# Every 16th output store of a gather, prefix-sum and matmul kernel goes out as two transfers, of 120 and of 8 partitions

## The chip, the core and the metric

The kernel runs on one core of a Trainium2 chip. The core has a matrix engine (PE, with its weight loads shown as PEld), a vector engine (DVE), a scalar engine (ACT), GpSimd (POOL) and a queue engine (SP) that here only issues transfers. The transfers themselves run on 16 DMA engines that all issuers share. Times are device microseconds (us) of one execution, and the figure that counts is the median over runs.

## The reference

```python
B, S, N, D = (16, 4096, 2048, 512)
# x: B x S x D float32, indices: B x N int64, sorted, w: D x D float32
b_idx = np.arange(B)[:, None]
gathered = x[b_idx, indices, :].copy()
cs = np.cumsum(gathered, axis=1)
return np.matmul(cs, w).astype(np.float32)
```

For each of 16 batches, 2048 rows of 512 floats are picked out of 4096, summed up along the rows (a running sum), and multiplied with a 512 x 512 matrix. 67.1 MB are gathered and 67.1 MB are written.

## The kernel before

The 16 x 2048 = 32768 gathered rows are cut into T = 256 tiles of 128 rows. Two tiles (R = 2) make a group, so there are G = 128 groups, 8 to a batch. A group's output is 256 rows of 2 KB, 512 KB.

The program is written by hand, engine by engine, with semaphores. The small class Lane (its method need waits on a semaphore only where that engine hasn't yet waited for as high a value) makes the waits. What follows is the way of one group.

GpSimd runs `gather(t)` for all 256 tiles, an indirect transfer that takes one row index per partition and brings 128 rows of 2 KB into `g32`. There are 16 such tile buffers (NG = 16, each with its own semaphore `s_g`), so a gather waits only for the cast of 8 groups before (`s_c`).

ACT runs `cast(g)` (L121), which turns a gathered group into float16, and `drain(g)` (L180), which copies a projected group out of PSUM into one of NO = 8 output buffers `ob`. Casts run three groups ahead of drains: cast(g + 3), drain(g), cast(g + 4), drain(g + 1) and so on. `drain(g)` waits for the store of the group 8 before it (`s_o`), so that the buffer is free, and for the projection (`s_b`).

PE runs `sums(t)` (L132), which makes the running sums inside a tile by multiplying with a triangle of ones, and `project(g, j)` (L168), the product with w. DVE runs `carry(t)` (L152, L147), which adds the last sum of the tile before and writes float16.

SP runs `store(g)` (L186) for all groups in order. It waits for `drain(g)` through `s_e` and issues one transfer of 128 partitions, 4 KB each, from `ob`. At the end SP waits for the last 8 stores. The order of the stores on SP and of the drains on ACT is the order of the groups. A transfer adds 16 in all to its semaphore when it has landed, which is why the waits count in sixteens.

The lines around the change, in short:

```python
def drain(g):
    act.need(s_o[g % NO], 16 * (g // NO))
    act.need(s_b, R * (g + 1))
    nc.scalar.copy(out=ob[g % NO][:], in_=pb[g % NB][:]).then_inc(s_e, 1)
...
    dst = out[b, h * R * P : (h + 1) * R * P, :].rearrange("(p j) d -> p j d", j=R)
    sp.need(s_e, g + 1)
    nc.sync.dma_start(out=dst, in_=ob[g % NO][:]).then_inc(s_o[g % NO], 16)
```

With j = R = 2, partition p holds the output rows 2p and 2p + 1 of the group, which lie one behind the other in memory: 4 KB in one piece for each partition.

Of the kernel before, what the change touches and what calls it, by code (L numbers as in the profile page):

```python
# [27 lines left out]
def kernel(  # L28
# [7 lines left out]
    nc = tc.nc  # L36
# [8 lines left out]
    G = T // R  # L45
# [5 lines left out]
    NA = 4  # L51
    NB = 2
    NC = 4
    NO = 8
    LOOP = 4
    AH = 2
# [16 lines left out]
    g16 = [const.tile([P, R, D], FP16, name=f"g16_{i}") for i in range(NH)]  # L73
    cst = [const.tile([P, DC, R, P], FP16, name=f"cst{i}") for i in range(NC)]
    ob = [const.tile([P, R, D], FP32, name=f"ob{i}") for i in range(NO)]
    pa = [ps.tile([P, DC, R, Q], FP32, name=f"pa{i}") for i in range(NA)]
# [4 lines left out]
    def sem(name):  # L81
        return tc.alloc_semaphore(name)
# [5 lines left out]
    s_g = [sem(f"s_g{i}") for i in range(NG)]  # L88
    s_o = [sem(f"s_o{i}") for i in range(NO)]
    s_c = sem("s_c")  # L90
    s_a = sem("s_a")
    s_d = sem("s_d")
    s_b = sem("s_b")
# [2 lines left out]
    pool, pe, dve, act, sp = (  # L96
        Lane(e) for e in (nc.gpsimd, nc.tensor, nc.vector, nc.scalar, nc.sync)
    )
# [42 lines left out]
    def carry(t):  # L141
        g, r = divmod(t, R)
        dve.need(s_b, R * (g - NC + 1))
        dve.need(s_a, t + 1)
        dst = cst[g % NC][:, :, :, r * Q : (r + 1) * Q]
        if t % NT == 0:
            nc.vector.tensor_copy(out=dst, in_=pa[t % NA][:]).then_inc(s_d, 1)  # L147
            return
        e = (r - 1) % R
        last = cst[(t - 1) // R % NC][:, :, R - 1, e * Q + Q - 1 : e * Q + Q]  # L150
        dve.need(s_d, t)
# [7 lines left out]
    def project(g, j, first=0):  # L159
# [7 lines left out]
        for c in range(DC):  # L167
            mm = nc.tensor.matmul(  # L168
                out=pb[g % NB][:, j],
                lhsT=cst[g % NC][:, c, j, :],  # L170
                rhs=w16[:, c, :],
# [4 lines left out]

    def drain(g):
        act.need(s_o[g % NO], 16 * (g // NO))
        act.need(s_b, R * (g + 1))
        nc.scalar.copy(out=ob[g % NO][:], in_=pb[g % NB][:]).then_inc(s_e, 1)  # L180

    def store(g):
        b, h = divmod(g, GB)
        dst = out[b, h * R * P : (h + 1) * R * P, :].rearrange("(p j) d -> p j d", j=R)
        sp.need(s_e, g + 1)
        nc.sync.dma_start(out=dst, in_=ob[g % NO][:]).then_inc(s_o[g % NO], 16)  # L186


    with nc.allow_non_contiguous_dma(reason="a few indices, one per partition"):
        nc.sync.dma_start(  # L190
            out=idx_first[:],
            in_=indices[0, 0 : FIRST * P].bitcast(U32).rearrange("(t p w) -> p t w", p=P, w=2),
        ).then_inc(s_first, 16)
    idx_rows = indices.bitcast(U32).rearrange("b (t q) -> (b t) q", q=2 * P)
    for k in range(KI):
        nc.sync.dma_start(
            out=idx64[:, k, :], in_=idx_rows[k * P : (k + 1) * P, :]
        ).then_inc(s_idx[k], 16)
    nc.sync.dma_start(out=w32[:], in_=w.rearrange("(c p) d -> p c d", p=P)).then_inc(s_w, 16)
    for g in range(G):  # L200
        store(g)
    for g in range(G - NO, G):
        sp.need(s_o[g % NO], 16 * (g // NO + 1))


    nc.gpsimd.memset(ident[:], 1.0).then_inc(s_ut, 1)  # L206
# [3 lines left out]
        out=ident[:],  # L210
        in_=ident[:],
# [7 lines left out]
        out=ut[:],  # L219
        in_=ut[:],  # L220
# [14 lines left out]
    for k in range(KI):  # L235
# [3 lines left out]
            out=pb[k % NB][:, 0, :P], in_=idxf[:, k, :], identity=ident[:]  # L239
# [31 lines left out]
    for g in range(G):  # L271
        if g + AH + 1 < G:
            cast(g + AH + 1)
        drain(g)
# [30 lines left out]
```

## Time and profile before

| what | value |
|---|---|
| median of 6 runs | 350.95 us (350.22 to 352.24) |
| the profiled execution: its time / its span | 352.32 us / 350.6 us |
| PE busy | 299.7 us (85%) |
| ACT busy | 253.4 us (72%) |
| POOL busy | 243.4 us (69%) |
| DVE busy | 178.1 us (51%) |
| DMA queue of GpSimd's gathers (q0) | 20480 records, 67.13 MB, 49.3% of 16 engines' span |
| DMA queue of SP's transfers (q1) | 19520 records, 68.43 MB, 48.4% |
| clock granted to PE | 0.999 |

The span is the time from the first to the last instruction of the profiled execution; its own time is 1.7 us longer and is one of a spread of runs. The share of busy time of an engine is a mean over the whole span. The page's name for a group of instructions is its line, engine, operation and the buffers it writes and reads ("g<-in_x_dram,idxg" is a gather). A DMA record is one packet that one of the 16 engines moves: 4 KB of data for gathers and stores, or 4 B for the write to a semaphore. Records overlap by a few ns where an engine is never idle, so that shares can add up to slightly more than 100%.

### The profile page before, as it was taken

What the parts mean: (1) busy time and instruction counts of PE and PEld (TensorE: products, weight loads), DVE (VectorE), ACT (ScalarE), POOL (GpSimd) and SP (SyncE); (2) the same over time, 40 slices, a digit from 0 to 9 for tenths busy, and PEclk for the clock granted to TensorE, in tenths of its full rate; (3) what the DMA queues carried; (4) which work ended last, traced back from release to release, by engine and by line L of the source; (5) the groups of instructions that cost most, each with busy time, mean ns of one, the idle gap of its engine ahead of it and who ended that gap; (6) DMA issues with size and microseconds to landing.
All of it is one profiled execution on the core that took longest, in us unless ns stands there. A gap on an engine that the chain in (4) does not pass through costs nothing.

```text
span 350.6 us, 6009 instructions
## 1 busy us (share of the span) xinstructions
PE 299.7 (85%) x2050; PEld 149.7 (43%) x2050; DVE 178.1 (51%) x260; ACT 253.4 (72%) x258; POOL 243.4 (69%) x264
## 2 busy tenths in 40 slices
PE   0498898898899889898998888998898998898993
PEld 0253443444444444444444444444444444444441
DVE  1364554464555546455554555555554555555550
ACT  0874877787787787776877767878787786877873
POOL 6777777777777777777777777777777777776000
PEclk9999999999999999999999999999999999999999
DMA  6789999999999999999999999999999999999845
GB/s 220 225 279 354 395 411 414 415 412 420 407 418 414 410 415 409 416 415 411 416 416 415 415 410 408 406 414 405 417 414 416 414 415 406 411 417 416 356 193 239
DMA packets 40012, 135.66 MB, mean 387 GB/s; under 512 B 6464, under 2 KB 6720, under 8 KB 40000
## 3 DMA queue, kind: packets, MB, share of 16 engines
q0 software_dynamic: 20480, 67.13, 49.3%
q1 hardware_dynamic: 19520, 68.43, 48.4%
q14 instruction: 11, 0.09, 0.1%
q8 instruction: 1, 0.02, 0.0%
HBM read 68.42 MB, written 67.11 MB: 387 GB/s over the span
## 4 chain that ended last, share of the span: by engine, by line
POOL 46%; DMA 27%; issue 18%; ACT 4%; PE 3%; POOLq 0%; SPq 0%; ACTq 0%
POOL g L109 46%; DMA g<-in_x_dram,idxg 26%; ACT g L121 3%; PE pb L168 3%; DMA g<-in_x_dram,idx_first 1%; PE pa L132 1%; DMA idx_first<-in_indices_dram 1%; ACT w L268 0%; ACT L121 0%; ACT ob L180 0%; POOLq L229 0%; ACTq L23 0%; SPq L300 0%; SPq L79 0%
## 5 line engine op out<-in xcount | busy, mean ns | idle before, releaser
L109 POOL DMA_INDIRECT g<-in_x_dram,idxg x254 | 240.2, 946 | 77.4 <-issue 71.3
L168 PE MATMUL pb<-w,cst 128*128 128x512 f16 x1024 | 263.6, 380 | 0.0
L152 DVE TENSOR_TENSOR cst<-pa,cst 128x512 f16<-128x512 f32 x240 | 166.0, 692 | 139.4 <-PE pa L132 138.4
L121 ACT CAST g<-g 128x1024 f16<-128x1024 f32 x128 | 133.6, 1045 | 78.8 <-issue 75.8
L132 PE MATMUL pa<-ut,g 128*128 128x128 f16 x1024 | 100.9, 222 | 40.9 <-ACT g L121 40.3
L180 ACT COPY ob<-pb 128x1024 f32<-128x1024 f32 x128 | 128.7, 1006 | 4.7 <-PE pb L168 4.7
L132 PEld LDWEIGHTS pa<-ut,g 128*128 128x128 f16 x1024 | 70.0, 99 | 128.6 <-ACT g L121 95.9
L168 PEld LDWEIGHTS pb<-w,cst 128*128 128x128 f16 x1024 | 89.9, 98 | 61.8 <-issue 1.1
L147 DVE CAST cst<-pa 128x512 f16<-128x512 f32 x16 | 11.1, 691 | 20.4 <-PE pa L132 20.4
L121 ACT ACT_TABLE_LOAD x1 | 1.3, 1283 | 9.5 <-DMA g<-in_x_dram,idx_first 9.5
L238 PE MATMUL pb<-ident,idxf 128*128 128x128 f32 x2 | 0.7, 458 | 4.6 <-DVE idxf L234 4.6
L109 POOL DMA_INDIRECT g<-in_x_dram,idx_first x2 | 2.1, 1060 | 1.6 <-DMA idx_first<-in_indices_dram 1.2
L234 DVE CAST idxf<-idx 128x128 f32<-128x128 uint32 x2 | 0.5, 228 | 4.4 <-DMA idx<-in_indices_dram 4.2
L238 PEld LDWEIGHTS pb<-ident,idxf 128*128 128x128 f32 x2 | 0.4, 182 | 4.7 <-issue 4.6
L268 ACT CAST w<-w 128x2048 f16<-128x2048 f32 x1 | 1.9, 1892 | 0.0
L243 DVE CAST idxg<-pb 128x128 uint32<-128x128 f32 x2 | 0.6, 290 | 0.3 <-PE pb L238 0.3
L206 POOL MEMSET ident<- 128x128 f32 x1 | 0.2, 204 | 0.5 <-SPq L79 0.5
L209 POOL TENSOR_SCALAR_AFFINE_SELECT ident<-ident 128x128 f32<-128x128 f32 x1 | 0.3, 286 | 0.1
L289 POOL MEMSET const-float32-0.0<- 128x1 f32 x1 | 0.1, 98 | 0.3 <-issue 0.3
L218 POOL TENSOR_SCALAR_AFFINE_SELECT ut<-ut 128x128 f16<-128x128 f16 x1 | 0.3, 289 | 0.0
L207 POOL MEMSET ut<- 128x128 f16 x1 | 0.2, 204 | 0.0
L289 POOL MEMSET const-uint8-127<- 128x1 uint8 x1 | 0.1, 115 | 0.0
(2 smaller groups left out, 0.2 us busy)
## 6 DMA issues: line engine op xcount, KB each, us to landing
out_dram<-ob SPq DMA_DIRECT2D x128, 512.0 KB, 6.9
g<-in_x_dram,idxg POOLq DMA_INDIRECT x254, 11.1
w<-in_w_dram SPq DMA_DIRECT2D x1, 1024.0 KB, 5.6
idx<-in_indices_dram SPq DMA_DIRECT2D x2, 128.0 KB, 2.6
g<-in_x_dram,idx_first POOLq DMA_INDIRECT x2, 5.1
idx_first<-in_indices_dram SPq DMA_DIRECT2D x1, 2.0 KB, 1.9
```

The costliest lines, as they stand in the source:

```text
L109: nc.gpsimd.indirect_dma_start(out=g32[g % (NG // R)][:, r, :], out_offset=None, in_=x_flat, in_offset=bass.IndirectOffsetOnAxis(ap=ap, ax ...
L121: nc.scalar.copy(out=g16[g % NH][:], in_=g32[g % (NG // R)][:]).then_inc(s_c, 1)
L132: mm = nc.tensor.matmul(out=pa[t % NA][:, c], lhsT=g16[g % NH][:, r, c * P : (c + 1) * P], rhs=ut[:], start=(c == 0), stop=(c == DC - 1),)
L147: nc.vector.tensor_copy(out=dst, in_=pa[t % NA][:]).then_inc(s_d, 1)
L152: nc.vector.tensor_tensor(out=dst, in0=pa[t % NA][:], in1=last.unsqueeze(2).broadcast_to([P, DC, R, Q]), op=mybir.AluOpType.add,).then_inc ...
L168: mm = nc.tensor.matmul(out=pb[g % NB][:, j], lhsT=cst[g % NC][:, c, j, :], rhs=w16[:, c, :], start=(c == 0), stop=(c == DC - 1),)
L180: nc.scalar.copy(out=ob[g % NO][:], in_=pb[g % NB][:]).then_inc(s_e, 1)
L209: nc.gpsimd.affine_select(out=ident[:], in_=ident[:], compare_op=mybir.AluOpType.is_equal, fill=0.0, base=0, pattern=[[-1, P]], channel_mu ...
L234: nc.vector.tensor_copy(out=idxf[:, k, :], in_=idx64[:, k, 0::2]).then_inc(s_if, 1)
L238: nc.tensor.transpose(out=pb[k % NB][:, 0, :P], in_=idxf[:, k, :], identity=ident[:]).then_inc(s_pt, 1)
L243: nc.vector.tensor_copy(out=idxg[:, k, :], in_=pb[k % NB][:, 0, :P]).then_inc(s_prep, 1)
L268: nc.scalar.copy(out=w16[:], in_=w32[:]).then_inc(s_wc, 1)
```

## The change

The store of every 16th group (0, 16, ..., 112) is issued as two transfers: the first 120 partitions, 480 KB, count on the buffer's semaphore as before; the last 8 partitions, 32 KB, count on a new semaphore, `s_o2`. The drain that will overwrite such a buffer (groups 8, 24, ..., 120) waits for both, and SP waits for `s_o2` once more at the end. Bytes, buffers, and the other 120 stores stay as they are.

```diff
+    SPLIT = 16
+    CUT = 120
...
+    s_o2 = sem("s_half")
...
     def drain(g):
         act.need(s_o[g % NO], 16 * (g // NO))
+        if (g - NO) % SPLIT == 0:
+            act.need(s_o2, 16 * max(0, (g - NO) // SPLIT + 1))
         act.need(s_b, R * (g + 1))
...
         sp.need(s_e, g + 1)
-        nc.sync.dma_start(out=dst, in_=ob[g % NO][:]).then_inc(s_o[g % NO], 16)
+        src = ob[g % NO]
+        if g % SPLIT:
+            nc.sync.dma_start(out=dst, in_=src[:]).then_inc(s_o[g % NO], 16)
+        else:
+            nc.sync.dma_start(out=dst[:CUT], in_=src[:CUT]).then_inc(s_o[g % NO], 16)
+            nc.sync.dma_start(out=dst[CUT:], in_=src[CUT:]).then_inc(s_o2, 16)
...
     for g in range(G - NO, G):
         sp.need(s_o[g % NO], 16 * (g // NO + 1))
+    sp.need(s_o2, 16 * ((G - 1) // SPLIT + 1))
```

## The prediction

> **What bounds the kernel now.** I read the chain of waits first, cut to its last 29 us. Columns: start in us, length in us, what was running.
>
> ```profile
> 321.97 0.30 issue
> 322.27 16.23 DMA g<-in_x_dram,idxg
> 338.50 0.72 issue
> 339.23 1.05 ACT g L121
> ...
> 345.36 1.01 ACT ob L180
> ```
>
> The reader is to see that the last gather is issued at 322.27, needs 16.23 us to land, and that everything after it (cast, sums, projection, the last copy, the last store) takes 350.6 - 338.5 = 12.1 us. So the end is "last gather landed" plus a fixed tail. Before it the chain is a row of gathers on GpSimd; the page's group for them:
>
> ```profile
> L109 POOL DMA_INDIRECT g<-in_x_dram,idxg x254 | 240.2, 946 | 77.4 <-issue 71.3
> ```
>
> 946 ns busy and 0.30 us of issue make 1.25 us for each gather, and 3.2 + 255 x 1.25 = 322 is exactly where the last one is issued: GpSimd is never held up. Hence only the landing time of the last gather can move the end earlier, down to GpSimd's own pace. Next I read the list of DMA issues in six windows of 20 us (20:40, 60:80, 120:140, 180:200, 240:260, 300:320), for the stores in the first and last, then the gathers in all six; the last number is the median us from issue to landing.
>
> ```profile
> out_dram<-ob SPq DMA_DIRECT2D x8, 512.0 KB, 6.9
> out_dram<-ob SPq DMA_DIRECT2D x8, 512.0 KB, 6.8
> g<-in_x_dram,idxg POOLq DMA_INDIRECT x17, 6.8
> g<-in_x_dram,idxg POOLq DMA_INDIRECT x17, 8.4
> g<-in_x_dram,idxg POOLq DMA_INDIRECT x17, 10.0
> g<-in_x_dram,idxg POOLq DMA_INDIRECT x17, 12.3
> g<-in_x_dram,idxg POOLq DMA_INDIRECT x17, 14.7
> g<-in_x_dram,idxg POOLq DMA_INDIRECT x17, 16.5
> ```
>
> Stores keep their time, gathers fall behind by 9.7 us over 280 us: the gather queue gets a backlog. Then the DMA view of 45:300, where the load is steady, and of two windows near the end, 331:335 and 335:339 (records, MB, share of 16 engines):
>
> ```profile
> DMA packets 30521, 105.28 MB, mean 413 GB/s; under 512 B 4831, under 2 KB 4831, under 8 KB 30513
> ```
> ```profile
> DMA  1111097997998979972101011010011029999999
> ...
> q1 hardware_dynamic: 224, 0.83, 51.3%
> q0 software_dynamic: 16, 0.05, 3.3%
> ```
> ```profile
> q1 hardware_dynamic: 217, 0.76, 47.0%
> q0 software_dynamic: 14, 0.05, 2.8%
> ```
>
> 413 GB/s over 16 engines is 25.8 GB/s each, or 4096 B in 158.7 ns. The windows near the end carry the case. Gathers are still outstanding (the last lands at 338.5), yet their queue uses 3.3% and then 2.8% of 16 engines, half of ONE engine (1/32 is 3.1%), and between the bursts of stores the busy row falls to 0 and 1 tenths. One gather gives each engine 4 packets of 4 KB and one semaphore write (20480 gather records / 256 gathers / 16 engines = 5). 16 records in 4 us are 3.2 gathers, one per 1.25 us: a single engine, alternating gather and store packets, while fifteen have finished their gathers. In 327:338.5 that queue has 63 records, in 327:331 34, of which that engine at its rate makes 16; the other 18 are less than one last gather of the others. So the late engine had about 63 - 18 = 45 records, 9 gathers, 36 packets, left when the others were done: 36 x 158.7 ns = 5.7 us of work. With equal numbers of store packets between, that is 11 us in time, and a gather counts as landed only when all engines are done.
>
> **What the Trainium skill says.** (1) Page "DMA: Bandwidth & Descriptors", section "Latency and other measured facts": of the 16 engines, numbers 7 and 15 are usually slower in traces. The trace agrees that one is late; it has no engine numbers, so which one it is stays open. (2) Same page, "Why a DMA increments its semaphore by 16 and not by 1": a transfer uses the largest k up to 16 that divides the slowest dimension of both sides, for a transfer issued from SP on the lowest-numbered k engines; of the semaphore's 16, the missing 16 - k are written at once. For 128 partitions k is 16, and the trace agrees in count (6464 records under 512 B, less 4096 of the gathers and 256 of the first indices, are 2112 = 132 transfers x 16). For smaller k no run here shows it yet. (3) Same page, "Rules for kernel authors", advises against cutting a transfer into two halves, as both use the same engines; that speaks against a gain from cutting as such, not against moving load between engines.
>
> **The change part by part.** Stores 0, 16, ..., 112 are cut: 8 of 128.
> - Load of the engines. Uncut, each engine gets 128/16 = 8 packets per store. By (2), 120 partitions give k = 15, 8 packets on engines 0 to 14 and none on 15; 8 partitions give k = 8, one packet on engines 0 to 7. Over 8 stores: engine 15 loses 64 packets, 64 x 158.7 = 10.2 us of work; engines 0 to 7 gain 8, 1.27 us; 8 to 14 keep theirs. Store 0 is issued at 20.1 us, before the transfers are saturated, so about 7 x 0.159 = 1.1 us counts.
> - If 15 is the late engine, 10.2 us is more than the 5.7 it is behind. It stops being last; engines 0 to 7 are next, 1.1 us above the level of the others: 5.7 - 1.1 = 4.6 us gained.
> - Cross-check by queue. With all engines equal, a gather and its half store are 8 packets, 8 x 158.7 = 1270 ns, against 1250 ns of GpSimd: 20 ns are still lost per gather, over the 220 gathers from 45 us on 4.4 us. The last gather would then take 6.8 + 4.4 + 1.1 = 12.3 us in place of 16.23: 3.9 us gained. The two ways give 3.9 and 4.6; I take 4.5, nearer to the count of packets, because the 6.8 us of the first window still holds transfers of the start.
> - Bounds. At best the saturated 158.7 ns shrink once nobody waits, GpSimd's 1250 ns set the pace and no backlog grows: 6.8 + 1.1 = 7.9 us for the last gather, 8.3 us gained. At worst nothing is gained here (rivals below).
> - SP: 8 more transfers at 332 ns each (the SP group's duration) beside 299 us in which SP waits for L180. The second piece leaves 0.33 us later than the first. Nobody reads it but the copy 8 groups later. Cost 0; without that cover 2.7 us.
> - ACT: 8 more waits (g = 8, 24, ..., 120), each on a store issued 8 groups before, some 20 us, and landing in 7. Queued behind is the copy at L180 and through it PE's next projection. ACT is idle 0.6 to 0.8 us ahead of most casts. The wait is always met; a waiting instruction shows as 0.02 us in the chain (ACTq L23), so 8 x 0.02 = 0.2 us, hidden. If a wait did bite it would be by the 0.33 us of the second issue, 2.6 us in all.
> - Last wait on SP: the last cut store is number 112, out 35 us before the end. Cost 0.
>
> Sum against the profiled execution: span 350.6 - 4.5 = 346.1. Its own time was 352.32, 1.4 over the median of 350.95, so I apply the difference to the median: 350.95 - 4.5 = 346.4.
>
> **Rivals.**
> A. The late engine is one of 0 to 7 (7 is the other engine that the skill names). It keeps all its work and gets 7 to 8 packets more: 1.1 to 1.3 us later, last gather and end with it; 352.2, slower. It decides from two packets over a late engine on. For: the skill names 7 and 15 alike. Against: it says that both are slow, and here only one is; nothing in the trace excludes it.
> B. The late engine is one of 8 to 14, or its lag comes from other traffic (the instruction queue moves 11 packets, 0.09 MB, in the span) that falls on an engine not relieved. Load on it unchanged: 350.9, same.
> C. The 120 partitions go out on 8 engines instead of 15. Then 0 to 7 get 15 + 1 packets per cut store, 8 more: 10.2 us in all. Even with the late engine freed it is 10.2 - 5.7 = 4.5 us slower, 355.4. Against: the rule in (2).
> D. The 120 partitions are spread over all 16 engines anyway; then nothing is relieved or loaded by more than a few packets: within 0.5 us, same.
>
> **How the numbers follow.** Forecast 0.58; A 0.18; B 0.10; C 0.08; D 0.04; 0.02 for a small gain in another way. What a measurement of this kernel can tell from no change is about 0.3%, 1.05 us. Faster: 0.58 + 0.02 = 0.60. Slower: A + C = 0.26. Same: B + D = 0.14. The likeliest case has its own range, 342.5 (the bound of 8.3 us) to 348.0 (a gain of 3). Adding B, D and A reaches to 352.4 and leaves out C and the edges: about 0.85 held, so the range is 342.5 to 352.4.
>
> **What would show it.** Right: the gathers' time to landing grows to 11 to 13 us in 300:320 instead of 16.5; the last gather lands near 334; near the end the gather queue no longer runs at half of one engine alone for 11 us, but several engines finish within some 2 us. The issue list shows 120 stores of 512 KB, 8 of 480 and 8 of 32, and the store queue has fewer semaphore records (15 + 8 per cut store). GpSimd's 1.25 us and the tail of 12 us stay. Wrong: 16 or more us to landing at the end with one engine still alone (A, B), or eight engines busy with gathers at the end, half of 16 (C).

## The result, and the profile after

The changed kernel takes 352.71 us (median of 16 runs, 351.43 to 354.19) against 351.42 us of the kernel before (37 runs, 350.22 to 353.0). The ratio is 1.0038, with a 95% interval from 1.0026 to 1.0050: 1.3 us slower, 0.9 to 1.8. The forecast was 346.4, and the range ended at 352.4.

The pair of profiled executions can't show this. Their spans are 350.8 and 350.6 us, but the profiled execution of before, 352.32 us, was itself 0.9 us above its median, and two executions of one kernel differ by more. In the changed kernel's the last gather was issued 0.7 us later (322.97 instead of 322.27) and took 0.25 us less to land, so the loss isn't seen in it as a longer wait; it rests on the medians and on the experiments below. What the profile shows is what the change did and what it left alone. First the page of the changed kernel: the record counts, and the DMA issues (count, KB each, median us to landing).

```profile
DMA packets 40068, 135.66 MB, mean 387 GB/s; under 512 B 6520, under 2 KB 6776, under 8 KB 40056
...
out_dram<-ob SPq DMA_DIRECT2D x120, 512.0 KB, 6.9
g<-in_x_dram,idxg POOLq DMA_INDIRECT x254, 10.6
out_dram<-ob SPq DMA_DIRECT2D x8, 480.0 KB, 6.9
```

Records under 512 B went from 6464 to 6520, 56 more, 7 for each cut store. A store in one piece writes 16 semaphore records; 15 + 8 are 7 more. So, by these counts, the large piece ran on 15 engines and the small one on 8, and engine 15 (if a piece takes the lowest-numbered engines) was relieved of 64 packets. That much of the prediction happened. Now the gathers in 300:320 of the changed kernel, then its DMA view of 331:335 and of 335:339 (records, MB, share of 16 engines):

```profile
g<-in_x_dram,idxg POOLq DMA_INDIRECT x17, 16.0
```
```profile
DMA  7814413198998999999981100101101101079999
...
q1 hardware_dynamic: 233, 0.83, 51.5%
q0 software_dynamic: 15, 0.05, 3.1%
```
```profile
q1 hardware_dynamic: 242, 0.86, 53.4%
q0 software_dynamic: 16, 0.05, 3.1%
```

The reader is to see that nothing was cured. The gathers still need 16 us at the end, and from 331 to 339 their queue still runs at 3.1%, half of one engine. One engine is as alone as before: the engine that lost 64 packets was not the late one. The trace shows this in a second way. It keeps the time of each of the 16 increments by which a gather counts as landed, though not the engine that made it. Of the gathers that began to land from 300 to 330 us, the 15th increment came 2.2 us after the first and the 16th 11.9 us in the kernel before (medians); in the changed kernel they came after 1.6 and 10.8 us. Fifteen engines are together, and one is 9 to 10 us behind them. In the chain of waits the last gather needs 15.98 us, and the tail behind it is about as long as it was:

```profile
322.97 15.98 DMA g<-in_x_dram,idxg
338.95 0.44 issue
339.39 1.05 ACT g L124
...
345.52 1.01 ACT ob L185
```

### The profile page after: what moved, and what is told of

It reads as the page before. It is cut to its first block, busy times and chain, and to the rows that moved or that the text cites. A ratio compares the mean times of both kernels' runs of the same rounds, so it can differ in the third digit from the quotient of the medians.

```text
span 350.8 us, 6017 instructions
## 1 busy us (share of the span) xinstructions
PE 299.6 (85%) x2050; PEld 149.6 (43%) x2050; DVE 178.1 (51%) x260; ACT 253.2 (72%) x258; POOL 244.0 (70%) x264
## 2 busy tenths in 40 slices
DMA packets 40068, 135.66 MB, mean 387 GB/s; under 512 B 6520, under 2 KB 6776, under 8 KB 40056
## 4 chain that ended last, share of the span: by engine, by line
POOL 51%; DMA 24%; issue 18%; ACT 2%; PE 2%; POOLq 0%; DVE 0%; SPq 0%; ACTq 0%
POOL g L112 51%; DMA g<-in_x_dram,idxg 24%; ACT g L124 2%; PE pb L171 1%; DMA idx<-in_indices_dram 1%; ACT ob L185 0%; POOLq L240 0%; PE pb L249 0%; PE pa L135 0%; SPq L200 0%; DVE idxg L254 0%; DVE idxf L245 0%; ACTq L23 0%; SPq L311 0%; SPq L81 0%
```

## The experiments

All of them cut stores into other pieces. The method: by the rule under (2) of the prediction, a piece of n partitions goes to the largest number of engines up to 16 that divides n (15 for 120, 8 for 8; the semaphore records of every kernel below come out as this rule has them). If these are always the lowest-numbered engines, the sizes of the pieces choose which engines get more packets and which fewer. The sign of the answer then tells on which side of the boundary the late engine lies. The numbers 0 to 15 are names under that rule; the trace carries none. Since the runs below come from several chips, the argument also takes it that the same number is late on all of them. The pieces are set by one line, and the rest of the edit is the loop that issues them:

```diff
-    CUT = 120
+    PIECES = (112, 8, 8)
...
-            nc.sync.dma_start(out=dst[:CUT], in_=src[:CUT]).then_inc(s_o[g % NO], 16)
-            nc.sync.dma_start(out=dst[CUT:], in_=src[CUT:]).then_inc(s_o2, 16)
+            lo = 0
+            for n in PIECES:
+                nc.sync.dma_start(out=dst[lo : lo + n], in_=src[lo : lo + n]).then_inc(
+                    s_o[g % NO] if lo == 0 else s_o2, 16
+                )
+                lo += n
```

Where a store is said to be cut "every 16th", only the line PIECES differs from this version; the counts that wait for s_o2 follow the number of pieces.

**Two batches that tell nothing.** In the first eight runs, on two other chips, the kernel before itself took 455 to 456 us. There the granted clock was 0.88, the transfers of 45:300 ran at 308 to 313 GB/s instead of 413, and the end no longer hung on the last gather (the chain named mostly PE and sources outside the core). The kernels (64 + 64, 112 + 8 + 8, 112 + 7 + 7 + 2 and 112 + 4 x 4, each twice) came out between 449 and 460 us. Only 64 + 64 gave a ratio with an interval, 1.0014 to 1.0211 in the second batch, and the bound there isn't the one under test. What was expected of the first four:

> Every 16th store is cut into 64 + 64 partitions, so every engine keeps its 8 packets (plus one more 4-byte semaphore write). Theory A (the late engine is one of 0 to 7 and pays for its 8 extra packets): no change, within 0.2 us of the kernel before. Rival (the cut itself costs, through one more issue on SP, more semaphore writes or the waits on ACT): the same 1.3 us slower as the change.

> Every 16th store in pieces of 112, 8 and 8 partitions: engines 0 to 7 get 9 packets, 8 to 15 get 7. Theory A, late engine in 0 to 7: 8 packets more for it, 1.1 to 1.3 us slower. Rival, late engine in 8 to 15: 8 packets fewer, 1.3 us faster. Rival, the cut itself costs: two more transfers per cut store instead of one, 2.6 us slower.

> Every 16th store in pieces of 112, 7, 7 and 2 partitions: engines 0 and 1 get 10 packets, 2 to 6 get 9, 7 to 15 get 7. If the late engine is number 7: 8 packets fewer for it, 1.1 to 1.3 us faster, although three more transfers are issued per cut store. If it is one of 2 to 6: 16 packets more, 2.5 us slower; if 0 or 1: 24 more, 3.8 us slower. If the cut itself costs 1.3 us per piece: 3.9 us slower.

> Every 16th store in pieces of 112 and four times 4 partitions: engines 0 to 3 get 11 packets, 4 to 15 get 7. If the late engine is 4 to 7: 1.1 to 1.3 us faster. If it is 0 to 3: 32 packets more, 5 us slower. In both cases the 0.3 us that separates the issues of the pieces on SP costs nothing, as SP has 299 us of waiting.

And of the same four on the second chip:

> The 64 + 64 cut once more, on a chip whose transfers run at the 413 GB/s of the first profile. Theory A (the late engine is one of 0 to 7): no change, within 0.2 us. Rival (the cut itself costs): 1.3 us slower.

> 112 + 8 + 8 once more: engines 0 to 7 get 9 packets, 8 to 15 get 7. Late engine in 0 to 7: 1.1 to 1.3 us slower. Late engine in 8 to 15: 1.3 us faster. The cut itself costs: 2.6 us slower.

> 112 + 7 + 7 + 2 once more: engines 0 and 1 get 10 packets, 2 to 6 get 9, 7 to 15 get 7. Late engine is 7: 1.1 to 1.3 us faster. It is one of 2 to 6: 2.5 us slower; 0 or 1: 3.8 us slower. The cut itself costs 1.3 us per extra piece: 3.9 us slower.

> 112 + 4 x 4 once more: engines 0 to 3 get 11 packets, 4 to 15 get 7. Late engine in 4 to 7: 1.1 to 1.3 us faster. In 0 to 3: 5 us slower. The cut itself costs 1.3 us per extra piece: 5.2 us slower.

These runs answer none of them. The questions were asked again below, except 64 + 64, in whose place stands the cut into four pieces of 32. In those for 112 + 7 + 7 + 2 and in the first for 112 + 4 x 4 I counted the packets of the small pieces without the one that the large piece has lost: against a whole store's 8, the loaded engines get 8 (or 16) more over the kernel, not 16 (or 24), and 24, not 32.

**112 + 7 + 7 + 2, every 16th store.**

```diff
-    PIECES = (112, 8, 8)
+    PIECES = (112, 7, 7, 2)
```

> 112 + 7 + 7 + 2, on a chip where the kernel before takes its 351 us: engines 0 and 1 get 10 packets per cut store, 2 to 6 get 9, 7 to 15 get 7. Late engine is 7: 1.1 to 1.3 us faster, and the last gather's wait for one lone engine about 2 us shorter. Late engine in 2 to 6: 2.5 us slower; 0 or 1: 3.8 us slower. The cut itself costs 1.3 us per extra piece: 3.9 us slower.

Measured: 1.0053 (1.0033 to 1.0073), 1.9 us slower (1.2 to 2.6). Engines 7 to 15 lost 8 packets here, worth 1.3 us. With 24 further transfers at the 24 ns measured in the next experiment, 0.6 us, a late engine among them would still have made the kernel faster: 7, the rival's candidate, is excluded, and 15 with it. The expectation repeats the error of the earlier ones: "9" is one more than 8, so 8 packets over the kernel and 1.3 us, not 16 and 2.5. Read rightly, 2 to 6 give 1.3 us plus what the pieces cost; 0 or 1 give 2.5 plus that cost.

**How much does a piece cost? Every 4th store as four pieces of 32.** No load is moved. This edit and the next are against the kernel before; all pieces count on the buffer's own semaphore, and the waits for it follow their number.

```diff
+    SPLIT = 4
+    PIECES = (32, 32, 32, 32)
...
-        nc.sync.dma_start(out=dst, in_=ob[g % NO][:]).then_inc(s_o[g % NO], 16)
+        lo = 0
+        for n in [P] if g % SPLIT else PIECES:
+            nc.sync.dma_start(
+                out=dst[lo : lo + n], in_=ob[g % NO][lo : lo + n]
+            ).then_inc(s_o[g % NO], 16)
+            lo += n
```

> Every 4th store in four pieces of 32 partitions: 96 more transfers in the kernel, 12 times as many as the change adds, and no load moved: each engine keeps its 8 packets per store and gets 96 more 4-byte semaphore writes. All pieces count on the buffer's own semaphore, so ACT has no wait more than before. Theory A (load on a late engine among 0 to 7): at most 96 x 9 ns = 0.9 us slower, from the semaphore writes. Rival (each further transfer costs, some 0.13 to 0.16 us, and the late engine is one of 8 to 14, untouched by the change): 12 us or more slower.

Measured: 1.0065 (1.0035 to 1.0095), 2.3 us for 96 further transfers, 24 ns each (13 to 35). That is more than I expected from the 9 ns of a semaphore record, and far from 0.13 us: cutting as such can explain 8 x 24 ns = 0.2 us of the change's 1.3.

**112 + 8 + 8, every 4th store.** The same edit with other pieces.

```diff
-    PIECES = (32, 32, 32, 32)
+    PIECES = (112, 8, 8)
```

> Every 4th store (32 of them) in 112 + 8 + 8: engines 0 to 7 get 9 packets, 8 to 15 get 7, four times the dose of the run with 112 + 8 + 8. Theory A, late engine in 0 to 7: 32 packets more, 5.1 us slower. Late engine in 8 to 15: 32 packets fewer for it and engines 0 to 7 become as late as it was: between 0 and 2 us faster. Each further transfer costs 0.13 us: 64 of them, 8 us slower on top of either.

Measured: 1.0205 (1.0186 to 1.0224), 7.2 us slower, from three runs; a fourth took 372.4 us, 4% longer than these, and is left out. 32 packets are 5.1 us and 64 transfers at 24 ns are 1.5, 6.6 together. The late engine is one of 0 to 7; a late engine among 8 to 15 is excluded.

**112 + 4 x 4, every 16th store.**

```diff
-    PIECES = (112, 7, 7, 2)
+    PIECES = (112, 4, 4, 4, 4)
```

> Every 16th store in 112 + 4 x 4: engines 0 to 3 get 11 packets, 4 to 15 get 7. Late engine in 4 to 7: 8 packets fewer, 1.1 to 1.3 us faster. In 0 to 3: 24 packets more, 3.8 us slower. In 8 to 15 with each of the 32 further transfers costing 0.13 us: 4.2 - 1.3 = 2.9 us slower.

Measured: 0.9964 (0.9950 to 0.9978), 1.3 us faster, and measured a second time 0.9973 (0.9961 to 0.9986), 350.38 us, 1.0 us faster. What was expected of the second measurement:

> 112 + 4 x 4 once more, in another call: engines 0 to 3 get 11 packets, 4 to 15 get 7. If the late engine is number 4 on this chip too: 0.6 to 1.3 us faster. If another engine is late there, one of 0 to 3: 3.8 us slower or more.

The late engine is not among 0 to 3, which got 24 packets more. Of the versions that write the whole output this is the only one that beats both kernels. Its chain in the second measurement, and the issues on its page:

```profile
322.19 14.42 DMA g<-in_x_dram,idxg
336.61 0.45 issue
337.06 1.05 ACT g L124
...
343.19 1.01 ACT ob L185
```
```profile
out_dram<-ob SPq DMA_DIRECT2D x120, 512.0 KB, 7.3
...
out_dram<-ob SPq DMA_DIRECT2D x8, 448.0 KB
...
out_dram<-ob SPq DMA_DIRECT2D x32, 16.0 KB
```

The last gather needs 14.42 us instead of 16.23. And its DMA view of 331:335:

```profile
DMA  9889973331230332218999899999898330221103
...
q0 software_dynamic: 39, 0.12, 7.7%
```

Between the bursts of stores the busy row stands at 2 and 3 tenths, no longer 0 and 1, and the gather queue at 7.7%: several engines are behind with their gathers together. The increments say how many: the 14th, 15th and 16th come 5.2, 8.6 and 9.3 us after the first, where before only the 16th was far behind. Two engines have nearly caught up with the late one, by the numbering two of the loaded 0 to 3. A larger dose would make the loaded ones the last. What engines 4 to 15 lose in this way falls on four engines, three times as much on each. If the late one is 36 packets behind, the two meet at a dose of 9, worth 9 x 158.7 ns = 1.4 us. By this estimate the 1.0 to 1.3 us are nearly all that cutting stores can give under this rule.

**112 + 6 + 6 + 4 and 112 + 5 + 5 + 5 + 1, every 16th store.**

```diff
-    PIECES = (112, 4, 4, 4, 4)
+    PIECES = (112, 6, 6, 4)
```

> Every 16th store in 112 + 6 + 6 + 4: engines 0 to 3 get 10 packets, 4 and 5 get 9, 6 to 15 get 7 (8 uncut). Late engine is 6: 8 packets fewer, less 24 further transfers at 0.02 us: 0.8 to 1.3 us faster. It is 4 or 5: 8 packets more and the transfers, 1.3 to 1.8 us slower.

```diff
-    PIECES = (112, 6, 6, 4)
+    PIECES = (112, 5, 5, 5, 1)
```

> Every 16th store in 112 + 5 + 5 + 5 + 1: engine 0 gets 11 packets, 1 to 4 get 10, 5 to 15 get 7 (8 uncut). Late engine is 5 or 6: 8 packets fewer, less 32 further transfers at 0.02 us: 0.6 to 1.3 us faster. It is 4: 16 packets more and the transfers, 2.5 to 3.2 us slower.

Measured: 1.0045 (1.0027 to 1.0062), 1.6 us slower, and 1.0055 (1.0037 to 1.0073), 1.9 us slower (1.3 to 2.6). The first excludes 6, the second 5 and 6. Only number 4 is left: it gains packets in both, and loses them in 112 + 4 x 4. These two versions and the second measurement of 112 + 4 x 4 ran on one chip, so for that chip 4 follows without the runs on others. The second is less slow than the 2.5 to 3.2 us expected of number 4; that difference I can't explain. Its sign is what decides.

**120 + 4 + 4, every 16th store.** The change with one thing undone, the packet on engines 4 to 7.

```diff
-    PIECES = (112, 5, 5, 5, 1)
+    PIECES = (120, 4, 4)
```

> The change with its second piece cut again: 120 + 4 + 4. Engines 0 to 3 get 10 packets per cut store, 4 to 14 get 8 as before the change, 15 gets none. Theory (late engine is 4, slower through its one packet more): only the 16 further transfers at 0.02 us remain, 0 to 0.4 us slower. Rival (the cut, the extra waits on ACT or the relief of 15 make it slower): at least the 1.3 us of the change.

Measured: 1.0005 (0.9991 to 1.0019). With more transfers than the change, the same number of waits on ACT and the same relief of engine 15, the loss is gone: the interval ends at 1.0019, and that of the change begins at 1.0026. So it was the packet.

**Unloading the late engine fully.** This kernel leaves out partitions 32 to 127 of every 16th store, so its output is incomplete; it is there for its time alone.

```diff
-    PIECES = (120, 4, 4)
+    PIECES = (4, 4, 4, 4, 4, 4, 4, 4, 96)
...
-            for n in PIECES:
+            for n in PIECES[:-1]:
```

> Leaves out the output of partitions 32 to 127 of every 16th store; the other 32 go out as eight pieces of 4, on engines 0 to 3. These keep their 8 packets per cut store, 4 to 15 get none: 64 fewer each over the kernel. The late engine (4) is unloaded by 10.2 us as the prediction wanted it for 15. Theory: the bound passes to engines 0 to 3, which keep their 2048 packets: the 5.7 us of the prediction less 56 further transfers at 0.02 us, 4 to 5.7 us faster. Rival (the end is set by GpSimd, the total of bytes or the tail, and the late engine only looks like the cause): under 1.5 us faster; or, if all engines' load counts alike, 12/16 of 10.2 us, 7.6 us faster.

Measured: 345.75 us, 0.9840 (0.9813 to 0.9867), 5.6 us faster (4.7 to 6.6). Gathers in 300:320, the queue in 331:335, and the chain's end in this kernel:

```profile
g<-in_x_dram,idxg POOLq DMA_INDIRECT x17, 9.9
```
```profile
q0 software_dynamic: 6, 0.02, 1.0%
```
```profile
332.70 1.05 ACT g L124
...
338.83 1.01 ACT ob L185
```

The gathers at the end need 9.9 us instead of 16.5, their queue is all but empty after 331 (6 records in 4 us), and the last cast starts at 332.70 instead of 339.23. The lone engine's wait is gone for the most part: the 16th increment comes 4.8 us after the first instead of 11.9, the 15th after 2.6. Both rivals, under 1.5 us and 7.6 us, lie outside the interval. The gain fits a late engine that is relieved until others are last. The run takes 64 packets from 4 to 15 alike, and 2.3% of all bytes with them; that number 4 is the engine that counts is shown by the pieces above, not by this run.

## Why the prediction was wrong, step by step

- *One engine is late, by about 36 packets.* Right. The increments show one engine behind fifteen, by 9.7 us at the end; at one gather packet and one store packet in turn that is some 31 packets, an estimate like the 36. In 112 + 4 x 4 the late engine loses 8 and engines 0 to 3 gain 24, which brings them 32 packets closer; there two engines have nearly caught up.
- *The end follows the last gather, and GpSimd is not in the way.* Right: 14.42 us to landing ends the chain earlier, and with 9.9 us in 300:320 the span is 344.2.
- *120 partitions load 15 engines with 8 packets each, 8 partitions load 8 engines with one.* Right in number, by the 56 further semaphore records. The Trainium skill's rule for the count ("DMA: Bandwidth & Descriptors", "Why a DMA increments its semaphore by 16 and not by 1") agrees; that the lowest-numbered engines are taken fits every sign found here but isn't shown by the trace itself.
- *The late engine is number 15.* This is the step that failed, and the only one of weight. It rested on one sentence of the Trainium skill ("DMA: Bandwidth & Descriptors", "Latency and other measured facts"), that 7 and 15 are usually slower, and on nothing in the trace. Numbered by the rule for the pieces, the runs put it at 4. The change took 64 packets from an engine that nobody waited for and gave 8 to the one that everything waits for.
- *Rival A, one of engines 0 to 7, 1.1 to 1.3 us slower.* This is what happened, 1.3 us. Its mechanism and size held, its favourite number 7 did not: 8 packets x 158.7 ns are 1.27 us, and 8 further transfers at 24 ns another 0.2. Over all 37 runs the median of the kernel before is 0.47 us above that of the 6 runs shown with the prediction, which is why rival A's 352.2 came out as 352.7.
- *Freeing the late engine gains 5.7 us, less 1.1 for the engines loaded instead.* The 5.7 agrees with the 5.6 us (4.7 to 6.6) measured where the late engine was freed and no engine was loaded more. The cross-check by queue gives 16.23 - 6.8 - 4.4 = 5.0 us without that 1.1, which lies in the same interval; the run doesn't decide between the two.
- *Issue on SP and waits on ACT cost nothing.* Consistent with 120 + 4 + 4, which has both and is within 0.2% of before.

Open is why one engine is late at all. The traffic that rival B names is not the main reason: in the profile of before the instruction queue moves nothing between 59 and 134 us, and in that time the 16th increment falls further behind the 15th, from 0.7 us (gathers that began to land from 60 to 70) to 3.2 us (from 110 to 120). That the engine is slower packet by packet was not tried.

## What to carry to other kernels

When transfers saturate all engines, look at the end of the trace: a queue that ran at 1/32 there, while the rest of the row was empty, was one engine holding everybody up, and its lateness could be counted in packets. Before moving load, find out which engine it is with runs that load different sets; here 112 + 4 x 4 and 112 + 5 + 5 + 5 + 1 would have been enough, together with the price of a piece. A rule of thumb on the slow engine, used as if it were measured, turned a hoped-for gain of 4.5 us into a loss of 1.3. And pieces of 120 and 8 partitions did not load the engines evenly (23 semaphore records instead of 16), so an odd piece is a choice of engines.

## What the runs showed of the hardware that I had not expected

- The late engine was number 4 in the numbering above, where the Trainium skill, in the section named above, has 7 and 15. The runs on one chip pin it; those on two other chips agree with 4 without narrowing it down to one (0 to 6 on one, 4 to 7 on the other).
- A further transfer in a saturated queue cost 24 ns (13 to 35) when all engines took part, more than the 9 ns of its semaphore record.
- The late engine falls behind all through the kernel, not at the end alone: in the kernel before the 16th increment came 7.4 us after the first for gathers that began to land from 180 to 200 us, and 11.9 us from 300 us on.
- With 120 + 4 + 4 or 112 + 4 x 4 the late engine has no part in the small pieces, and there the pieces cost it nothing that can be measured (0.2 us slower, and 1.3 and 1.0 us faster where 8 packets fewer are worth 1.27). So the cost seems to lie on the engine that writes the semaphore; this was not tested by itself.
